# A float32 decoder on one Trainium2 core: half of retention's output product as block pairs, gates kept in HBM, head norms by quarters, and fourteen weight units with low parts from ScalarE and an accumulating transfer

## The chip, the cores and the metric

The kernel runs on one core of a Trainium2 chip. The metric is the device time of one execution in microseconds (us). TensorE is PE (its weight loads are PEld), VectorE is DVE, ScalarE is ACT, GpSimd is POOL, and SyncE, which issues most transfers, is SP.

## The reference

Two layers; 512 tokens; width 1024. The weights are float32. In each layer

```python
h = rmsnorm(x, g_mix)
aq, ak, av, rq, rk, rv, rg, ga, gb = split(h @ w_in)      # 5888 columns
A = sliding_window_attention(aq, ak, av, sinks)            # 8 heads, window 128
r = retention(rq, rk, rv)                                  # 4 heads of 256 columns
r = r * rsqrt(mean(r * r, per head) + EPS) * silu(rg)
mixed = sigmoid(ga) * (A @ w_a) + sigmoid(gb) * (r @ w_b)
x = x + mixed @ w_out
x = x + square(relu(rmsnorm(x, g_mlp) @ w_up)) @ w_down
```

and a last rmsnorm of x. The change touches r's norm, sigmoid(gb), r @ w_b, and how the weights of gb, w_b and w_out are prepared.

## The kernel before

**Layout and precision.** Activations stand transposed: a chunk is 128 features on partitions by 512 tokens. A matmul takes a 128x128 block of weights as its stationary side and 512 tokens as its moving side. Each float32 operand is split in two parts of a reduced format: `hi` is a rounded copy that ScalarE writes (L257), `lo` is the rest, raw minus hi, by VectorE (L258). A product then takes three matmuls, hi·hi, hi·lo and lo·hi (`products`, L303 to L305). PE pays three times for every product, and each weight costs one ACT and one DVE pass.

**Weight units.** All weights come in units of 128x1024 (512 KB), in the order that `unit_order` writes out. `load_until` issues the loads on SP three units ahead into `raw` tiles, `split_until` makes hi and lo, and `unit` hands a unit to the product that uses it and has the next ones split. The pool `wpool` holds three each of raw, hi and lo: a unit's hi and lo can be written only when the unit three before it has been read by its last matmul. PSUM has eight banks: five for `ps_mm` and three for `ps_aux`.

**Kinds of products.** `chunk` takes one unit and gives one output chunk: 8 blocks × 3 = 24 matmuls of 512 columns. `group` takes four units and gives four chunks together in four banks: 96 matmuls of 512. `two_chunks` takes two units for two chunks. `narrow_pair` (L563) gives two output chunks from two weight units by seven block products instead of eight: the units' halves and sums and differences of them (`load_part` and `add_part`, which make four parts, on DVE) meet halves of the input and sums and differences of those (`sum_input`, `form_of`: "forms"). Each of its seven products has 4 blocks × 3 matmuls over 256 tokens, 84 matmuls of 256 columns in all. Before the change, w_out's last six chunks and most of w_up's are made as pairs.

**Retention and gates.** `retention(pair)` is a generator that runs in the background of the projection chunks: `advance` lets it take a step at fixed points (twice a chunk, times a rate). Per head it makes scores, outputs, a norm (`inverse_rms`, L405: a matmul with ones sums the squares, ACT takes the root of 128x512, DVE the reciprocal of 128x512) and `finish` (L996), which multiplies by the norm and by silu(rg) and splits the result into the moving side of w_b. The queue's order after retention's second half is: rg chunks 4–7; gates 0–3 (`chunk` with `gate`, L835: DVE multiplies by rstd, ACT takes the sigmoid); the w_b `group` for chunks 0–3; gates 4–7; w_b chunks 4–7; w_out `two_chunks`; w_out's pairs; then w_up. `put_mixed` (L1088) multiplies w_b's output by the gate, adds the attention branch and splits the sum. `chunk` order within the gates is permuted by CROSSED, so that pairs of chunks lie beside each other.

**Order.** The program is written in this order, and a scheduler settles the order of instructions on each engine when the kernel is built. Each engine then runs its list in order and waits at an instruction whose operands aren't there, with all behind it.

Of the kernel before, what the change touches and what calls it, by code (L numbers as in the profile page):

```python
# [18 lines left out]
P = 128  # L19
# [33 lines left out]
BETWEEN = (0, 2, 4, 5)  # L53
H = T // 2
CROSSED = (0, 1, 4, 5, 2, 3, 6, 7)


def unit_order():

    def plain(name, *at):  # L60
        return [(name, i) for i in range(*at)]

    def pairs(src, *firsts):
        return [("pair", j, part, src) for j in firsts for part in range(4)]

    order = plain("w_in", 26) + plain("w_a", 4) + plain("w_in", 26, 42)
    order += plain("w_b", 4) + plain("w_in", 42, 46) + plain("w_b", 4, 8)
    order += plain("w_out", 2) + pairs("w_out", 2, 4, 6)
    for what, q, i in mlp_sequence():
        if what == "first":  # L70
            order += plain("w_up", 4)
        elif what == "pair":
            order += pairs("w_up", 8 * q + 2 * i)
        elif what == "down":
            order += plain("w_down", 8 * q + 2 * i, 8 * q + 2 * i + 2)
        else:
            order += plain("w_down", 8 * q, 8 * q + 8)
    return order
# [43 lines left out]
def view(slot):  # L122
    return slot[0][:, slot[1], :]
# [3 lines left out]
def decoder(ctx, tc, xT, x_first, w_in, w_a, w_b, w_out, w_up, w_down, tables, decay, band, triangles, g_last, out):  # L127
# [33 lines left out]
    xhl = const.tile([P, 2, KD, T], F32R, name="xhl")  # L161
    xh, xl = xhl[:, 0], xhl[:, 1]
    slots = Slots([const.tile([P, 4, T], F32R, name=f"r{i}") for i in range(10)])
    spill = dram.tile([P, KD, T], F32, name="spill")


    order = [(layer, *u) for layer in range(DEPTH) for u in unit_order()]
    raws, parts, homes = {}, {}, []
    state = {"next": 0, "loaded": 0, "split": 0}

    def halves(i):

        return (slice(0, UNIT // 2), slice(UNIT // 2, UNIT)) if i < 3 else (slice(0, UNIT),)
# [59 lines left out]
    def split_until(n):  # L233
        while state["split"] < min(n, len(order)):
            i = state["split"]
            load_until(i + 3)
            paired = order[i][1] == "pair"
            if paired:
                add_part(i)
            raw = raws[i]  # L240
            if homes and i >= len(order) - len(homes):
                home = homes[len(order) - 1 - i]
                hi, lo = (home[:, 2 * a : 2 * a + 2, :].rearrange("p a t -> p (a t)") for a in range(2))
            else:


                first = (ASIDE, ASIDE) if paired else (0, 0)
                if paired and order[i][4] == "w_up" and wide(order[i][2]):
                    first = (ASIDE, 0)
                hi, lo = (  # L250
                    wpool.tile([P, UNIT + P], F32R, tag=n, name=n)[:, a : a + UNIT] for n, a in zip(("hi", "lo"), first)
                )
            for at in (LEFT,) if paired and order[i][3] == 3 else halves(i):
                if i == 0 and at.start == 0:
                    nc.vector.tensor_copy(hi[:, at], raw[:, at])
                else:
                    nc.scalar.activation(hi[:, at], raw[:, at], AF.Copy)  # L257
                last_low[:] = [nc.vector.tensor_tensor(lo[:, at], raw[:, at], f32(hi[:, at]), ALU.subtract).ins]  # L258
# [57 lines left out]
    xs = [(xh[:, k, :], xl[:, k, :]) for k in range(KD)]  # L316

    background = []
    credit = [0.0]
# [70 lines left out]
    def sum_parts(acc, folded=True):  # L390
# [11 lines left out]
        split(sh, sl, acc)  # L402
        return [sh, sl]

    def inverse_rms(both, n, dest):  # L405

        ps = bank(ps_aux, "ssq")
        for i, part in enumerate(both):
            nc.tensor.matmul(ps, ones, part, start=i == 0, stop=i == len(both) - 1)
        nc.scalar.activation(dest, ps, AF.Sqrt, bias=eps, scale=1.0 / n)  # L410
        nc.vector.reciprocal(dest, dest)
# [2 lines left out]

    def scaled_input(k, which):

        split(xh[:, k, :], xl[:, k, :], x[:, k, :], gain[:, which * KD + k : which * KD + k + 1])

    def squared_input(k, which):
        if k == 0:  # L420
# [94 lines left out]
    def layer_body(layer):  # L515
# [40 lines left out]

        def block(half, tokens):
            at = slice(tokens * H, tokens * H + H)
            return [xhl[:, :, k, at] for k in range(4 * half, 4 * half + 4)]

        FIRST, SECOND = slice(0, H), slice(H, T)

# [310 lines left out]
        def values(pair):  # L873

            banks = [bank(ps_mm, "rv") for _ in range(NB)]
            for u in range(4):
                hi, lo = unit("w_in", layer)
                for j in range(2):
                    k = 2 * u + j
                    cols = slice(j * T, (j + 1) * T)  # L880
                    for b, ps in enumerate(banks):
                        at = slice(b * P, (b + 1) * P)
                        products(
                            ps, [((xh[:, k, at], xl[:, k, at]), (hi[:, cols], lo[:, cols]))], k == 0, k == KD - 1
                        )
# [6 lines left out]
        rg, rg_next = {}, {}  # L892

        def put_rg(i):
            def put(ps):
                if i % 2 == 0:
                    two = big("z")
# [22 lines left out]
        class Head:  # L920
# [85 lines left out]
        def retention(pair):  # L1006
# [23 lines left out]
            for head in two:  # L1030
                head.finish()
                yield

        qk(0, PACE)
        for i in range(4):
# [36 lines left out]
        gates, gate_tiles = [], []  # L1072

        def gate_tile(c):
            if c % 2 == 0:
                two = big("gb")
                gate_tiles.append(two)
                gates.extend(two[:, j, :] for j in range(2))
# [7 lines left out]
        ms = {}  # L1086

        def put_mixed(c):  # L1088
            def put(ps):
                m = gates[c]  # L1090
                nc.vector.tensor_tensor(m, ps, m, ALU.mult)
                nc.vector.tensor_tensor(m, m, mixed[CROSSED[c]], ALU.add)
                hi, lo = slots.one(), slots.one()
                split(view(hi), view(lo), m)
                ms[CROSSED[c]] = (hi, lo)
# [22 lines left out]
        source = xT if layer == 0 else spill  # L1118
        for c in range(KD):
            nc.sync.dma_start(x[:, c, :], source[:, c, :])  # L1120

        def next_input(c):
            scaled_input(c, g_mlp)
# [63 lines left out]
        def wide_pair(first, close, pool, step):  # L1187
# [30 lines left out]
            part = unit("pair", layer)  # L1218
            multiply(a, part, True, block(0, 0))
            if first:  # L1220
                nc.tensor.matmul(b, part[0][:, :P], xh[:, 0, :], start=True, stop=True)
# [69 lines left out]
        for what, q, i in mlp_sequence():  # L1291
            if what == "first":
                late = group("w_up", layer, xs, [put_up] * 4, first_hooks())
            elif what == "pair":
                pair(q, i, late)
                if (q, i) == (3, 3):
                    for t, _ in homes_x:
                        slots.give(*t[1])
            elif what == "down":
# [3 lines left out]
            elif layer == DEPTH - 1:  # L1303
                end(layer, up[q])
            else:
                all_of(group("w_down", layer, up[q], [put_down(c, True) for c in range(4)]))
                for c in range(4, KD):
                    chunk("w_down", layer, up[q], put_down(c, True))
                slots.give(*up_slots[q])

    scaled_input(0, 0)
    split_until(1)
    for u in (2, 3):
# [77 lines left out]
    return units + [_swapped(u) if i % 2 else u for i, u in enumerate(_units_chunks(w, 2 * P + r(D - 2 * P)))]  # L1391


def _up_units(w):

    units = _units_group(w, np.arange(T))
# [51 lines left out]
def _laid_out(x, g_mix, w_in, sinks, w_a, w_b, w_out, g_mlp, w_up, w_down, g_final):  # L1448
# [13 lines left out]
        "w_b": _stack(w_b, lambda w: _half_grouped(w[:, _crossed(r(D))])),  # L1462
# [27 lines left out]
```

## Time and profile before

| | us |
|---|---|
| median of 3 runs | 1479.55 |
| lowest and highest | 1479.36, 1480.13 |
| profiled execution | 1479.77 |
| its span | 1478.0 |
| PE busy in it | 1469.1 |
| ACT busy | 786.5 |

The profile is of one execution. A row of the windows view gives busy time of each engine in a stretch, with the number of instructions. A row of the timeline gives start, duration, engine, line, operation, out<-in and shapes; `[0.55 <-PE mm]` at its end is idle time before it and what ended it. Matmuls overlap one another, so their pace is read from start to start, not from the durations. In groups the figures behind the bar are total busy time, mean of one in ns, and the idle time before them with its releasers. In the transfers' rows the last figure is the median from issue to landing.

### The profile page before, as it was taken

To read this page: it belongs to the slowest core of one execution; us is meant where nothing else is said; L and a number is where in the kernel's file an instruction comes from. 1 tells how busy PE (TensorE), PEld (TensorE's weight loads), DVE (VectorE), ACT (ScalarE), POOL (GpSimd) and SP (SyncE) were. 2 spreads that over 40 slices of the span, in tenths; PEclk is the share of its full clock that TensorE was granted. 3 is DMA by queue.
4 is the path that set the end of the run, shared out by engine and by line. 5 is a ranking of instruction groups with operands and counts; after the bars stand their busy time and mean duration, and the time that the engine had idled before them with its cause. 6 is when DMAs were issued, how large, how long until landed. Compare 5 with 4: busy or idle time off the path is not lost.

```text
span 1478.0 us, 19499 instructions
## 1 busy us (share of the span) xinstructions
PE 1469.1 (99%) x7322; PEld 1245.8 (84%) x7322; DVE 1144.0 (77%) x1864; ACT 786.5 (53%) x1250; POOL 3.8 (0%) x14
## 2 busy tenths in 40 slices
PE   9999999999999999999999999999999999999998
PEld 7888888888988888888888888888889888888887
DVE  7998668776998787776678975786779977878763
ACT  7656355643674445444456743556347654444553
POOL 0000000000000000000000000000000000000000
PEclk9999999999999999999999999999999999999999
DMA  6422322244323332333543233232433333333341
GB/s 226 136 86 86 93 82 89 75 125 128 92 81 114 100 114 93 105 103 114 167 129 91 86 98 87 87 100 76 135 93 105 102 95 99 115 103 110 90 140 57
DMA packets 52845, 155.58 MB, mean 105 GB/s; under 512 B 6416, under 2 KB 6544, under 8 KB 52752
## 3 DMA queue, kind: packets, MB, share of 16 engines
q1 hardware_dynamic: 52464, 153.83, 33.8%
q8 instruction: 57, 0.93, 0.3%
q10 hardware_dynamic: 288, 0.52, 0.1%
q14 instruction: 36, 0.29, 0.1%
HBM read 147.51 MB, written 4.19 MB: 103 GB/s over the span
## 4 chain that ended last, share of the span: by engine, by line
PE 91%; issue 5%; DVE 3%; DMA 1%; ACT 0%; POOLq 0%; SPq 0%; DVEq 0%
PE mm L305 21%; PE mm L303 21%; PE mm L304 21%; PE mm L1196 10%; PE mm L1197 5%; PE rv L303 2%; PE rv L305 2%; PE rv L304 2%; DVE lo L258 1%; PE score L776 1%; PE r L303 1%; PE r L305 1%; PE r L304 1%; PE pT L731 0%; PE pv L758 0%
## 5 line engine op out<-in xcount | busy, mean ns | idle before, releaser
L257 ACT ACTIVATE hi<-raw 128x1024 fp32r<-128x1024 f32 (+1 forms) x326 | 327.8, 1006 | 410.3 <-PE mm L304 210.9
L258 DVE TENSOR_TENSOR lo<-raw,hi 128x1024 fp32r<-128x1024 f32 (+1 forms) x327 | 377.6, 1156 | 125.9 <-ACT hi L257 122.4
L304 PE MATMUL mm<-r,hi 128*128 128x512 f32 (+1 forms) x824 | 298.6, 363 | 0.0
L303 PE MATMUL mm<-r,hi 128*128 128x512 f32 (+1 forms) x824 | 295.2, 364 | 0.0
L305 PE MATMUL mm<-r,lo 128*128 128x512 f32 (+1 forms) x824 | 293.3, 363 | 1.3 <-DVE lo L258 1.2
L304 PE MATMUL mm<-xhl,hi 128*128 128x512 f32 (+1 forms) x696 | 268.4, 388 | 0.0
L303 PE MATMUL mm<-xhl,hi 128*128 128x512 f32 (+1 forms) x696 | 268.2, 387 | 0.0
L305 PE MATMUL mm<-xhl,lo 128*128 128x512 f32 (+1 forms) x696 | 265.2, 388 | 0.0
L305 PEld LDWEIGHTS mm<-r,lo 128*128 128x128 f32 x824 | 154.1, 188 | 27.3 <-DVE lo L258 2.5
L304 PEld LDWEIGHTS mm<-r,hi 128*128 128x128 f32 x824 | 154.6, 188 | 23.9
L303 PEld LDWEIGHTS mm<-r,hi 128*128 128x128 f32 x824 | 154.2, 188 | 24.3
L303 PEld LDWEIGHTS mm<-xhl,hi 128*128 128x128 f32 x696 | 130.7, 188 | 25.6 <-ACT xhl L313 0.5
L305 PEld LDWEIGHTS mm<-xhl,lo 128*128 128x128 f32 x696 | 130.7, 188 | 24.7
L304 PEld LDWEIGHTS mm<-xhl,hi 128*128 128x128 f32 x696 | 130.8, 188 | 24.5
L1196 PE MATMUL mm<-r,hi 128*128 128x512 f32 x416 | 146.4, 391 | 0.0
L1197 PE MATMUL mm<-r,lo 128*128 128x256 f32 x416 | 115.4, 277 | 0.3 <-DVE lo L258 0.2
L1196 PE MATMUL mm<-xhl,hi 128*128 128x512 f32 x312 | 110.1, 391 | 0.0
L1196 PEld LDWEIGHTS mm<-r,hi 128*128 128x128 f32 x416 | 78.1, 188 | 16.3
L1197 PE MATMUL mm<-xhl,lo 128*128 128x256 f32 x312 | 86.6, 278 | 0.9 <-DVE lo L258 0.9
L1197 PEld LDWEIGHTS mm<-r,lo 128*128 128x128 f32 x416 | 78.1, 188 | 2.4 <-DVE lo L258 1.2
L1196 PEld LDWEIGHTS mm<-xhl,hi 128*128 128x128 f32 x312 | 58.6, 188 | 12.0
L1197 PEld LDWEIGHTS mm<-xhl,lo 128*128 128x128 f32 x312 | 58.6, 188 | 2.8 <-DVE lo L258 1.6
(261 smaller groups left out, 2051.9 us busy)
## 6 DMA issues: line engine op xcount, KB each, us to landing
raw<-w_in_in SPq DMA_DIRECT2D x89, 512.0 KB, 3.6
raw<-w_down_in SPq DMA_DIRECT2D x64, 512.0 KB, 3.6
raw<-w_up_in SPq DMA_DIRECT2D x36, 512.0 KB, 3.6
raw<-w_up_in SPq DMA_DIRECT2D x56, 256.0 KB, 2.8
raw<-w_b_in SPq DMA_DIRECT2D x16, 512.0 KB, 3.6
raw<-w_out_in SPq DMA_DIRECT2D x10, 512.0 KB, 3.6
raw<-w_a_in SPq DMA_DIRECT2D x8, 512.0 KB, 3.5
x<-xT_in SPq DMA_DIRECT2D x15, 256.0 KB, 3.1
```

The lines of the kernel that those rows point to most:

```text
L257: nc.scalar.activation(hi[:, at], raw[:, at], AF.Copy)
L258: last_low[:] = [nc.vector.tensor_tensor(lo[:, at], raw[:, at], f32(hi[:, at]), ALU.subtract).ins]
L303: nc.tensor.matmul(ps, ah, bh, start=start and i == 0, stop=False, **more)
L304: nc.tensor.matmul(ps, ah, bl, start=False, stop=False, **more)
L305: nc.tensor.matmul(ps, al, bh, start=False, stop=stop and i == n - 1, **more)
L776: nc.tensor.matmul(ps[:, g * w : (g + 1) * w], q_s[g][:, c, at], part[:, keys], start=i == 0, stop=i == 1)
L1196: nc.tensor.matmul(both, hi[:, c], m, start=start and k == 0, stop=False, **more)
L1197: nc.tensor.matmul(ps[:, :H], lo[:, c], m[:, 0, :], start=False, stop=k == 3 and start, **more)
```

## The change

- **w_b chunks 0–3** are made as two block pairs with `narrow_pair` (`mixed_pair`) in place of the `group`. Their forms of r are summed when each half of retention is finished.
- **Gates**: all eight gate chunks come before w_b, at an advance rate of 1.25. Two at a time they are written to HBM (`aside`) and read back when w_b uses them.
- **The tile `xhl`**, constant before, becomes slots that are given back after the gates and taken again.
- **Head norms**: `inverse_rms_apart` takes a head's root as four pieces of 32x128 on ACT, the reciprocal of one 128x128, writes the row of 512 to HBM, and reads it back spread over 128 partitions.
- **ADDED units**: for the gates' eight units, w_b 4–7 and w_out 0–1, ACT writes hi, then lo = −hi; then a transfer that POOL issues adds the weight from HBM to lo. DVE's subtraction is dropped. These weights are read from HBM twice.

```diff
+ADDED = {"w_b": range(4, 8), "w_in": range(38, 46), "w_out": range(2)}
...
-    order = plain("w_in", 26) + plain("w_a", 4) + plain("w_in", 26, 42)
-    order += plain("w_b", 4) + plain("w_in", 42, 46) + plain("w_b", 4, 8)
+    order = plain("w_in", 26) + plain("w_a", 4) + plain("w_in", 26, 46)
+    order += pairs("w_b", 0, 2) + plain("w_b", 4, 8)
     order += plain("w_out", 2) + pairs("w_out", 2, 4, 6)
...
+            if adds(i):
+                nc.scalar.activation(hi, raw, AF.Copy)
+                last_low[:] = [nc.scalar.activation(lo, f32(hi), AF.Copy, scale=-1.0).ins]
+                nc.gpsimd.dma_start(lo, weights[order[i][1]][order[i][0], order[i][2]], accum_op=ALU.add)
+                raws.pop(i)
+                parts[i] = (hi, lo)
+                state["split"] += 1
+                continue
...
+    def inverse_rms_apart(both, n, dest):
+
+        ps = bank(ps_aux, "ssq")
+        for i, part in enumerate(both):
+            nc.tensor.matmul(ps, ones, part, start=i == 0, stop=i == len(both) - 1)
+        own = temp("own")[:, :P]
+        for b in range(NB):
+            rows, cols = slice(32 * b, 32 * b + 32), slice(b * P, (b + 1) * P)
+            nc.scalar.activation(own[rows, :], ps[rows, cols], AF.Sqrt, bias=eps[rows, :], scale=1.0 / n)
+        nc.vector.reciprocal(own, own)
+        row = dram.tile([NB, P], F32, tag="row", name="row", bufs=2)
+        nc.sync.dma_start(row, own[0 : P : P // NB, :])
+        nc.sync.dma_start(dest, row.rearrange("b t -> (b t)").unsqueeze(0).broadcast_to([P, T]))
...
-                inverse_rms(self.parts, RET_V, self.inv)
+                inverse_rms_apart(self.parts, RET_V, self.inv)
...
+            for i in (pair, pair + 2):
+                homes_r[i] = forms_home()
+                by_form_r[i] = homes_r[i][1]
+            sum_input(by_form_r, [rg_tiles[2 * pair], rg_tiles[2 * pair + 1]], 2 * pair)
...
         for i in range(4, 8):
-            chunk("w_in", layer, xs, put_rg(i))
...
-        for c in range(4):
-            gate_tile(c)
-            chunk("w_in", layer, xs, gate(gates[c]))
+            chunk("w_in", layer, xs, put_rg(i), 1.25)
+        gates, gate_tiles, fresh = [], [], []
+
+        def put_aside(c):
+            def put(ps):
+                if c % 2 == 0:
+                    fresh[:] = [big("gb")]
+                gate(fresh[0][:, c % 2, :])(ps)
+                if c % 2:
+                    nc.sync.dma_start(aside[:, c - 1 : c + 1, :], fresh[0])
+
+            return put
+
+        for c in range(KD):
+            chunk("w_in", layer, xs, put_aside(c), 1.25)
         drain()
+        old_input()
+
+        def gate_tile():
+            c = len(gates)
+            two = big("gate")
+            nc.sync.dma_start(two, aside[:, c : c + 2, :])
+            gate_tiles.append(two)
+            gates.extend(two[:, j, :] for j in range(2))
...
-        all_of(group("w_b", layer, rT, [put_mixed(c) for c in range(4)]))
+
+        def mixed_pair(c):
+
+            gate_tile()
+            two, own = gate_tiles[c // 2], CROSSED[c]
+
+            def put(i, at, src, z):
+                return nc.vector.tensor_tensor(two[:, i, at], two[:, i, at], src, ALU.mult)
+
+            narrow_pair(ps_aux if c == 0 else ps_mm, lambda ins: None, form_of(by_form_r), block_r, put)
+            nc.vector.tensor_tensor(two, two, x[:, own : own + 2, :], ALU.add)
+            for i in range(2):
+                split_mixed(c + i, gates[c + i])
...
+        for c in (0, 2):
+            mixed_pair(c)
+        for t, _ in homes_r:
+            slots.give(*t[1])
...
         for c in range(4, KD):
-            gate_tile(c)
-            chunk("w_in", layer, xs, gate(gates[c]))
-        for c in range(4, KD):
+            if c % 2 == 0:
+                gate_tile()
             chunk("w_b", layer, rT, put_mixed(c))
```

More of the change, by code (lines that the diff above doesn't have):

```diff
@@ L160, in decoder @@
     x = little_x[:, P:].rearrange("p (k t) -> p k t", t=T)
[L161 to L164, printed above, removed]
+    slots = Slots([const.tile([P, 4, T], F32R, name=f"r{i}") for i in range(14)])
+    spill, aside = (dram.tile([P, KD, T], F32, name=n) for n in ("spill", "aside"))
     order = [(layer, *u) for layer in range(DEPTH) for u in unit_order()]
@@ L169, in decoder, with adds @@
     state = {"next": 0, "loaded": 0, "split": 0}
+    def adds(i):
+        return order[i][1] in ADDED and order[i][2] in ADDED[order[i][1]]
     def halves(i):
@@ L314, in split, with new_input, old_input @@
             nc.vector.scalar_tensor_tensor(lo, src, scale, f32(hi), ALU.mult, ALU.subtract)
-    xs = [(xh[:, k, :], xl[:, k, :]) for k in range(KD)]
+    xs, x_homes = [], []
+    def new_input():
+        x_homes[:] = [slots.four() for _ in range(KD // 2)]
+        xs[:] = [(x_homes[k // 2][0][:, k % 2, :], x_homes[k // 2][0][:, 2 + k % 2, :]) for k in range(KD)]
+    def old_input():
+        for t in x_homes:
+            slots.give(*t[1])
     background = []
@@ L415, in scaled_input @@
     def scaled_input(k, which):
-        split(xh[:, k, :], xl[:, k, :], x[:, k, :], gain[:, which * KD + k : which * KD + k + 1])
+        split(*xs[k], x[:, k, :], gain[:, which * KD + k : which * KD + k + 1])
     def squared_input(k, which):
@@ L558, in block @@
             at = slice(tokens * H, tokens * H + H)
-            return [xhl[:, :, k, at] for k in range(4 * half, 4 * half + 4)]
+            return [x_homes[k // 2][0][:, k % 2 :: 2, at] for k in range(4 * half, 4 * half + 4)]
         FIRST, SECOND = slice(0, H), slice(H, T)
@@ L896, in put @@
                 if i % 2 == 0:
-                    two = big("z")
+                    two = rg_tiles[i // 2] = big("z")
                     rg[i], rg_next[i + 1] = two[:, 0, :], two[:, 1, :]
@@ L1070, in layer_body, with split_mixed @@
         for i in range(4, 8):
-            chunk("w_in", layer, xs, put_rg(i))
[L1072 to L1078, printed above, removed]
-        for c in range(4):
-            gate_tile(c)
-            chunk("w_in", layer, xs, gate(gates[c]))
-        drain()
+            chunk("w_in", layer, xs, put_rg(i), 1.25)
[10 more added lines that the diff above has]
+            chunk("w_in", layer, xs, put_aside(c), 1.25)
+        drain()
+        old_input()
[5 more added lines that the diff above has]
+            gates.extend(two[:, j, :] for j in range(2))
         ms = {}
+        def split_mixed(c, m):
+            hi, lo = slots.one(), slots.one()
+            split(view(hi), view(lo), m)
+            ms[CROSSED[c]] = (hi, lo)
         def put_mixed(c):
@@ L1092, in put, with block_r @@
                 nc.vector.tensor_tensor(m, m, mixed[CROSSED[c]], ALU.add)
-                hi, lo = slots.one(), slots.one()
-                split(view(hi), view(lo), m)
-                ms[CROSSED[c]] = (hi, lo)
+                split_mixed(c, m)
             return put
         rT = [tuple(view(s) for s in ret[k]) for k in range(KD)]
-        all_of(group("w_b", layer, rT, [put_mixed(c) for c in range(4)]))
+        def mixed_pair(c):
[7 more added lines that the diff above has]
+                split_mixed(c + i, gates[c + i])
+        def block_r(half, tokens):
+            at = slice(tokens * H, tokens * H + H)
+            return [tuple(m[:, at] for m in rT[CROSSED[k]]) for k in range(4 * half, 4 * half + 4)]
+        for c in (0, 2):
+            mixed_pair(c)
+        for t, _ in homes_r:
+            slots.give(*t[1])
         homes_m = [forms_home(), None, forms_home(), None]
@@ L1220, in wide_pair @@
             if first:
-                nc.tensor.matmul(b, part[0][:, :P], xh[:, 0, :], start=True, stop=True)
+                nc.tensor.matmul(b, part[0][:, :P], xs[0][0], start=True, stop=True)
             ins = nc.vector.tensor_copy(b, a).ins if close else nc.scalar.activation(b, a, AF.Copy).ins
@@ L1461, in _laid_out @@
         "w_a": _stack(w_a, lambda w: _units_chunks(w[wa_rows], r(D))),
-        "w_b": _stack(w_b, lambda w: _half_grouped(w[:, _crossed(r(D))])),
+        "w_b": _stack(w_b, _ret_units),
         "w_out": _stack(w_out, _out_units),
```

13 lines of the change are left out of this document (11 added, 2 removed).

## The prediction

> **What bounds the kernel now.** First the page: busy times and the summary of the chain that ended last.
>
> ```profile
> span 1478.0 us, 19499 instructions
> PE 1469.1 (99%) x7322; PEld 1245.8 (84%) x7322; DVE 1144.0 (77%) x1864; ACT 786.5 (53%) x1250; POOL 3.8 (0%) x14
> PE 91%; issue 5%; DVE 3%; DMA 1%; ACT 0%; POOLq 0%; SPq 0%; DVEq 0%
> ```
>
> TensorE works 99% of the span, so time goes down by fewer PE microseconds and up by every new PE wait. POOL does nothing. Then PE's waits, and the busy times by stage in layer 0: the matmuls of w_b's group (296.5 to 318), gates 4–7 (to 340), w_b 4–7 (to 362), w_out.
>
> ```profile
> PE mm L305 <- DVE lo L258: 1.2, 2, 0.6
> PE mm L1197 <- DVE lo L258: 1.1, 3, 0.5
> ```
> ```profile
> 296.50:318.00 21.50, 21.50 (x96) 17.83 (x95) 12.31 (x12) 7.75 (x9) 0.00 (x0) 1.00 0.32 97
> 318.00:340.00 22.00, 22.00 (x98) 18.21 (x97) 18.58 (x25) 11.40 (x14) 0.00 (x0) 1.00 0.53 158
> 340.00:362.00 22.00, 22.00 (x98) 18.20 (x97) 13.09 (x17) 6.67 (x8) 0.00 (x0) 1.00 0.34 103
> 382.00:392.00 10.00, 9.69 (x83) 9.48 (x81) 10.00 (x16) 6.94 (x12) 0.00 (x0) 1.00 0.26 60
> 392.00:402.00 10.00, 9.72 (x81) 9.61 (x82) 9.96 (x17) 6.18 (x11) 0.00 (x0) 1.00 0.44 146
> ```
>
> PE waits only 2.3 us, always for a low part (`lo`) of a weight from VectorE. The columns are PE, PEld, DVE, ACT, POOL busy, clock (1.00, undisturbed), DMA share and GB/s. Where w_b and the gates run, PE is full and DVE has room; only in w_out's block pairs is DVE full. The changed stage is bounded by PE, with some 9 us of DVE slack in 21.5.
>
> **The matmuls (a gain).** The rates come from PE's timeline at the end of w_out's pairs and in w_up:
>
> ```profile
> 399.74 0.28 PE L303 MATMUL mm<-r,hi 128*128 128x256 f32 x1
> ...
> 402.21 0.40 PE L303 MATMUL mm<-xhl,hi 128*128 128x512 f32 x1
> ...
> 405.21 0.39 PE L304 MATMUL mm<-xhl,hi 128*128 128x512 f32 x1
> ...
> 407.02 0.39 PE L303 MATMUL mm<-xhl,hi 128*128 128x512 f32 x1
> ```
>
> From 399.74 to 402.21 lie 21 matmuls of 256 columns: 0.1176 us each, start to start. From 405.21 to 407.02 lie 8 of 512: 0.2263. Per layer the change removes the group's 4 units × 2 × 4 × 3 = 96 of 512 (21.7 us) and adds 2 pairs × 7 products × 4 blocks × 3 = 168 of 256 (19.8 us). Gain 1.95 a layer, **−3.9** in all. The number of gate matmuls doesn't change.
>
> **Work that moves off or onto idle time.** The groups by form:
>
> ```profile
> L258 DVE TENSOR_TENSOR lo<-raw,hi 128x1024 fp32r<-128x1024 f32 x287 | 350.5, 1221 | 122.3 <-ACT hi L257 118.8 <-PE ret L305 2.4
> L311 DVE TENSOR_TENSOR r<-z,r 128x512 fp32r<-128x512 f32 x64 | 42.9, 686 | 2.8 <-ACT r L310 2.6
> L411 DVE RECIPROCAL inv<-inv 128x512 f32<-128x512 f32 x8 | 26.8, 3353 | 10.4 <-ACT inv L410 10.4
> L257 ACT ACTIVATE hi<-raw 128x1024 fp32r<-128x1024 f32 x287 | 303.7, 1058 | 398.0 <-PE mm L304 208.9 <-PE mm L1196 101.2 <-issue 50.6
> ```
>
> - Fourteen units a layer lose DVE's subtraction (14 × 1.22 = 17 us off DVE) and gain a second ScalarE copy (14 × 1.06 = 15 us on ACT). Eight gates and six others take 76 us of PE; ACT worked about half of that stage (11.40 of 22.00), so per unit of 24 × 0.2263 = 5.4 us it carries two copies and a sigmoid, under 3 us. Nothing by itself; its cover is ACT's idle half.
> - The pairs add DVE sums (four 128x512 of weights and some of `r` per pair, under 0.7 each). They fit into the slack above, except at one place (below).
> - Gates to HBM and back: four writes and four reads of 512 KB a layer on SP. In the new order the first read stands behind the write of gates 4–5 and is wanted after the first pair's fourth product, by my count 4 us after it has landed at 3.6 us a piece. Nothing; if that cover went, DVE's gate product would come late and the PSUM bank after it.
>
> **Norms by a quarter and through HBM (a small loss).** The rows beside it: the old chain of a head, and the transfers.
>
> ```profile
> 301.45 0.69 ACT L410 ACTIVATE inv<-ssq,x 128x512 f32<-128x512 f32 x1 [2.10 <-PE ssq L409]
> 302.18 3.35 DVE L411 RECIPROCAL inv<-inv 128x512 f32<-128x512 f32 x1 [3.39 <-ACT inv L410]
> ...
> 306.52 1.28 DVE L1000 TENSOR_TENSOR z<-z,inv 128x512 f32<-128x512 f32 x2
> 307.72 1.29 DVE L1001 TENSOR_TENSOR z<-rr,z 128x512 f32<-128x512 f32 x2
> 308.93 1.22 DVE L258 TENSOR_TENSOR lo<-raw,hi 128x1024 fp32r<-128x1024 f32 x1
> 310.06 1.28 DVE L311 TENSOR_TENSOR r<-z,r 128x512 fp32r<-128x512 f32 x2
> ```
> ```profile
> raw<-w_up_in SPq DMA_DIRECT2D x56, 256.0 KB, 2.8
> raw<-w_b_in SPq DMA_DIRECT2D x16, 512.0 KB, 3.6
> spill<-x SPq DMA_DIRECT2D x8, 256.0 KB, 2.3
> x<-spill SPq DMA_DIRECT2D x8, 256.0 KB, 3.0
> r<-r SPq DMA_DIRECT2D x8, 64.0 KB, 3.6
> ```
>
> Start to start, DVE steps cost 0.60 (306.52 to 307.72 holds two of 512) and 1.13 (308.93 to 310.06; I count 1.15) for 1024. Old: 0.7 + 3.4 = 4 us. New, estimated: four roots (1.9), a quarter of the reciprocal (3.35/4 = 0.84) with a weight sum ahead of it, done 3.5 us after the square sum; the row to HBM like `spill<-x`, 2.3; back like `x<-spill`, 3.0: landed at 9. DVE stands in its order at the multiplication by it, and behind that wait the last head's seven steps, four gates' evacuations (the last gate's PSUM bank waits for the first of these) and the low parts of the first pair. In layer 0's new order the last square sum stands 64 matmuls ahead of gate 7 and 87 (19.7 us) ahead of the first pair's first low part. From 9 on, in DVE's new order: the head's seven steps and gate 2's evacuation, 8 × 0.60, so its bank is free at 13.8 (wanted at 14.3); five more of 0.60 and 1.15 give the first `lo` at 17.95 (wanted 19.7); two of each kind the second at 21.5 (22.5); the third, behind a form's low part, two sums and ScalarE's copy of them, at 26.2 (25.3: 0.9 late); the second pair's first, behind three of 0.60 and two of 256 columns at 0.33 (446.18 to 446.51, below), at 29.8 (28.2 + 0.9: another 0.75). So 1.7 in layer 0. In layer 1 the square sum stands 13 matmuls, 3 us, earlier: nothing. **+1.7**, between 0 (a trip shorter by 1 us does it) and 4.2 (both ways like `r<-r`, 7.2 in place of 5.3: +1.9 in layer 0, +0.6 in layer 1). I take the rows of 256 KB to and from HBM: the same two directions; a row of 2 KB that is spread over 128 partitions is nearest to them in what lands.
>
> **Low parts by an accumulating transfer (the disputed term).** Nothing in this trace runs such a transfer. Its nearest scene is where pairs of w_up give way to a plain unit:
>
> ```profile
> 442.89 1.05 ACT L257 ACTIVATE hi<-raw 128x1024 fp32r<-128x1024 f32 x1
> ...
> 445.04 1.22 DVE L258 TENSOR_TENSOR lo<-raw,hi 128x1024 fp32r<-128x1024 f32 x1
> ...
> 445.08 0.28 PE L1197 MATMUL mm<-xhl,lo 128*128 128x256 f32 x1
> ...
> 445.19 0.40 PE L303 MATMUL mm<-r,hi 128*128 128x512 f32 x1
> ...
> 445.28 1.06 ACT L257 ACTIVATE hi<-raw 128x1024 fp32r<-128x1024 f32 x1 [0.55 <-PE mm L1196]
> ...
> 445.89 0.40 PE L304 MATMUL mm<-r,hi 128*128 128x512 f32 x1
> 446.18 0.42 DVE L1208 TENSOR_TENSOR eu<-eu,mm 128x256 f32<-128x256 f32 x1
> ...
> 446.32 0.73 PE L305 MATMUL mm<-r,lo 128*128 128x512 f32 x2
> 446.51 0.42 DVE L1203 TENSOR_TENSOR z<-mm,side 128x256 f32<-128x256 f32 x1
> ```
>
> Here a low part took 3.4 us from the start of its high part (442.89) to its first use (446.32), and PE still waited 0.2 (445.89 + 0.23 to 446.32). The change makes such a scene behind the second pair of w_b: unit w_b 4 takes the buffers of that pair's second weight part. In the new order PE then has 36 matmuls of 256 and four of 512 ahead of w_b 4's first low part: 36 × 0.1176 + 4 × 0.2263 = 5.1 us. Off go 0.2 to start (445.28 above followed a matmul begun at 445.08), two copies of 1.06: 2.8 us are left for a transfer of 512 KB from issue to landing, X. The PE stall is X − 2.8, once a layer, in both.
>
> X from below: a plain 512 KB load, 3.6, stall 0.8. A second stream through the engines (the target is read too) costs what 256 KB more cost, twice: 2 × (3.6 − 2.8) = 1.6, so 5.2. In the order the raw load of the next unit is issued about 1 us earlier, another 512 KB: partly shared, +0.8. I take **X = 6.0**, stall 3.2, **+6.4** in all. From above: two plain loads end to end and the shared one, 2 × 3.6 + 1.6 = 8.8: 6.0 a layer, 12.0.
>
> The Trainium skill ("DMA: Bandwidth & Descriptors", the section "Anatomy of one DMA — SWDGE (gpsimd) path") gives transfers issued from GpSimd 2.0 us and bytes at 436 GB/s, an estimate of 3.2 us for 512 KB, below every plain row here; by it the sum would be 1478.4 in place of 1484.0.
>
> The other thirteen units have slack: three `lo` buffers turn over in 3 × 5.4 = 16.3 us, of which one unit's reading (5.4) and ACT (2.4) take 7.8, so X up to 8.5 costs nothing.
>
> **Sum.** Against the profiled execution's own 1479.8 (span 1478.0 and 1.8 around it, 0.2 above the median): 1479.8 − 3.9 + 1.7 + 6.4 = 1484.0; against the median 1483.8.
>
> **Rivals.**
> 1. *The transfer lands as fast as a plain load* (X under 4.5). For it: POOL and its queue are idle and the stage's DMA share is 0.34. Against it: each word is read twice. At X = 3.6: 1479.8 − 3.9 + 1.7 + 1.6 = 1479.2, not slower; without the norm's stall 1477.5. If DVE, freed of six subtractions just before w_out, also loses the pairs' wait there (0.6 a time by the waits, two times), 1476.3. It decides below X = 2.8 + 1.95 = 4.75, where a layer's stall eats its gain. Chance 0.30, of which 0.12 ends faster.
> 2. *The transfer is slow and all fourteen units starve* (X of 9 and more), because descriptors or the add run late. At X = 10: 7.2 behind the pairs, and (7.8 + 10 − 16.3)/3 = 0.5 for each of 8 gates, 11.2 a layer: 1479.8 − 3.9 + 1.7 + 22.4 = 1500. For it: nothing here shows a POOL transfer, and DVE is 84% busy in the gates' stage (18.58 of 22). Against it: a plain load is far below. Chance 0.10. The Trainium skill ("SBUF — State Buffer", the trap "DVE blocks DMA") has VectorE's two-port operations hold up the writing of such descriptors; no run shows it yet.
> 3. *The norm's trip is long, and DVE becomes the bound in front of the pairs*: both ways like `r<-r` (4.2), and the second pair's weights, whose buffer DVE frees late, land 1.6 later a layer (3.2): 1479.8 − 3.9 + 7.4 + 6.4 = 1489.7. For it: VectorE waits in order. Against it: the margins above are near 0.5 to 2 us only in layer 0. Chance 0.08.
> 4. *The change doesn't do what it says*: the pairs' PE gain is lost because PEld (9.5 of 10 in pairs) paces them. Against it: 0.1176 was measured there. With it 1487.9; chance 0.04.
>
> **How the numbers follow.** The forecast (X from 4.5 to 7.5) has 0.48 and its own range is 1481 to 1487. About 0.2%, 3 us, is what a measurement here can tell: faster means below 1476.6, slower above 1482.5. Faster: 0.12 of rival 1 and 0.03 of the forecast's with DVE's relief and no norm stall, 0.15. Same: the rest of rival 1 (0.18) and the forecast where X is below 5.2 (0.10), 0.28. Slower: 0.57. The range takes in rival 1's lower end and X = 8.8 (1479.8 − 3.9 + 1.7 + 12.0 = 1489.6): 1476.0 to 1490.0, leaving out rival 2 and slivers of the others.
>
> **What would show it.** Right: a PE wait of 2 to 5 us once a layer at w_b 4's first low matmul, released by a POOL transfer; 256-wide steps of 0.118 in the new pairs; PE's waits on `lo` elsewhere under 2 us a layer; 28 POOL transfers landing 5 to 7 us after issue. Wrong: no PE wait there (rival 1), waits at each gate unit (rival 2), or long PE waits for DVE's `lo` in the first pair (rival 3).

## The result, and the profile after

The changed kernel takes 1500.3 us (median of 4 runs, 1498.0 to 1504.4) against 1479.6 (4 runs, 1479.4 to 1480.1): ratio 1.0141, interval 1.0128 to 1.0154. It is 20.7 us slower. The forecast, 1483.8, had the sign right and a fifth of the size. The new kernel's runs also spread over 6 us, the old one's over less than 1.

The page of the changed kernel, its busy times, the summary of the chain that ended last and two rows of the transfer queues (packets, MB, share of the sixteen engines' span):

```profile
span 1500.4 us, 20088 instructions
PE 1474.7 (98%) x7466; PEld 1253.5 (84%) x7466; DVE 1132.8 (76%) x1892; ACT 837.9 (56%) x1330; POOL 28.1 (2%) x42
PE 84%; issue 7%; DVE 5%; DMA 3%; ACT 1%; POOLq 0%; SPq 0%; DVEq 0%; ACTq 0%
q1 hardware_dynamic: 56560, 164.33, 34.1%
q0 software_dynamic: 4032, 14.68, 5.8%
```

Transfers now hold 3% of the chain. The software queue is the 28 adding transfers: 14.68 MB, 5.8% of 1500.4 us of all sixteen engines, 3.1 us for each 512 KB. The hardware queue moved 164.33 MB in 34.1%, 1.6 us for each 512 KB. A transfer that adds took about twice the engines' time of a plain one.

What PE waited for (total us, times, longest):

```profile
PE mm L316 <- DMA lo<-w_b_in: 9.6, 2, 5.4
PE mm L314 <- DVE gb L871: 3.3, 2, 2.3
PE mm L316 <- DVE lo L269: 1.7, 4, 0.6
PE mm L314 <- ACT hi L268: 1.6, 1, 1.6
...
PE mm L316 <- DMA lo<-w_in_in: 0.2, 1, 0.2
```

Two long waits for w_b 4's low part, one a layer, as forecast; two for gates' evacuations by DVE and one for a first-pair weight, all where the last head's norm makes its trip; almost none at the gate units.

The transfers, median from issue to landing:

```profile
lo<-w_in_in POOLq DMA_DIRECT2D x16, 512.0 KB, 6.6
...
gate<-aside SPq DMA_DIRECT2D x8, 512.0 KB, 8.8
lo<-w_b_in POOLq DMA_DIRECT2D x8, 512.0 KB, 9.0
...
raw<-w_out_in SPq DMA_DIRECT2D x12, 256.0 KB, 12.8
...
inv<-row SPq DMA_DIRECT2D x8, 256.0 KB, 4.0
```

The trace has the landing of every POOL transfer, but of few that SP issued, so three of these rows rest on little: `gate<-aside` on two reads (4.8 us for a first pair's, 12.8 beside the adding transfers), `raw<-w_out_in` on three loads (12.8 and 13.2 behind the pairs, 3.2 later), `inv<-row` on one. Even so the loads of w_out's pairs, which nobody changed and whose median was 3.1 us before, took four times as long behind w_b's pairs. Not all of that comes from the adding transfers: with none of them (the first experiment below) two such loads took 6.8 and 7.8 us. Now the place behind the second pair in layer 0, from POOL's and PE's timelines:

```profile
341.95 0.86 POOL L259 DMA_DIRECT2D lo<-w_b_in  x1 [35.85 <-ACT lo L258]
344.62 0.86 POOL L259 DMA_DIRECT2D lo<-w_b_in  x1 [1.81 <-ACT lo L258]
346.97 0.86 POOL L259 DMA_DIRECT2D lo<-w_b_in  x1 [1.48 <-ACT lo L258]
```
```profile
344.53 0.40 PE L315 MATMUL mm<-r,hi 128*128 128x512 f32 x1
350.33 0.80 PE L316 MATMUL mm<-r,lo 128*128 128x512 f32 x1 [5.41 <-DMA lo<-w_b_in]
350.92 0.63 PE L314 MATMUL mm<-r,hi 128*128 128x512 f32 x1
351.35 0.63 PE L315 MATMUL mm<-r,hi 128*128 128x512 f32 x1
351.78 0.63 PE L316 MATMUL mm<-r,lo 128*128 128x512 f32 x1
```

Issued at 341.95, used at 350.33: X was 8.4 us. PE stood from 344.53 + 0.23 for 5.6 us. In layer 1 X was 8.4 us as well; there PE stood 0.9 us for a high part by ScalarE and then 4.4 for the low part. Then something new: from 350.92 the matmuls start 0.43 us apart in place of 0.23. The windows of the same stretch show it in the last column but two, the granted clock (with DMA share and GB/s behind it):

```profile
340.00:344.00 4.00, 3.95 (x32) 3.51 (x32) 2.82 (x6) 3.42 (x4) 0.86 (x1) 1.00 0.89 267
344.00:348.00 4.00, 0.93 (x6) 0.48 (x5) 3.44 (x5) 3.77 (x6) 1.73 (x2) 0.94 0.97 237
348.00:352.00 4.00, 1.67 (x4) 1.39 (x5) 3.58 (x5) 1.61 (x2) 0.00 (x0) 0.50 1.05 270
352.00:356.00 4.00, 4.00 (x14) 3.12 (x14) 0.00 (x0) 0.00 (x0) 0.00 (x0) 0.71 1.05 273
```

The clock falls to 0.50 after the wait, and the sixteen DMA engines are all busy (0.89 to 1.05, where the stage was at 0.34 before).

**Where 22.4 us of span went.** Over all matmuls behind the start, counted at the two paces of the prediction: the new shapes are 3.9 us less; starts that came late add 29.7 us where they added 9.4 before; 31 matmuls at 0.43 add 0.2 each, 6.2. Sum −3.9 + 20.3 + 6.2 = 22.6.

The second place, the norm's trip of the last head in layer 0, as PE, DVE and SP saw it:

```profile
299.19 0.39 PE L429 MATMUL ssq<-sh,ones 128*128 128x512 f32 x1
```
```profile
303.15 0.69 DVE L226 TENSOR_TENSOR raw<-raw 128x512 f32<-128x512 f32 x1 [5.38 <-DMA raw<-w_b_in]
303.76 0.95 DVE L434 RECIPROCAL own<-own 128x128 f32<-128x128 f32 x1
311.48 1.29 DVE L1034 TENSOR_TENSOR z<-z,inv 128x512 f32<-128x512 f32 x2 [6.78 <-DMA inv<-row]
```
```profile
304.73 0.50 SPq L436 DMA_DIRECT2D row<-own  x1
306.46 0.32 SPq L437 DMA_DIRECT2D inv<-row  x1
```

12.3 us from square sum to use, not 9.0: the sum of the first pair's weights, ahead of the reciprocal on DVE, waited for its load (about 2 us), and the way back took 5.0, not 3.0. In layer 1 it was 15.1 us. The DMA engines were 0.83 and 0.84 busy during the two trips. PE then stood 1.8 and 1.2 us in layer 0, and 2.5 in layer 1, for banks and weights that DVE gave late.

### The profile page after: what moved, and what is told of

Its sections match the earlier page's. It is cut to its first block, busy times and chain, and to the rows that moved or that the text cites. A ratio compares the mean times of both kernels' runs of the same rounds, so it can differ in the third digit from the quotient of the medians.

```text
span 1500.4 us, 20088 instructions
## 1 busy us (share of the span) xinstructions
PE 1474.7 (98%) x7466; PEld 1253.5 (84%) x7466; DVE 1132.8 (76%) x1892; ACT 837.9 (56%) x1330; POOL 28.1 (2%) x42
## 3 DMA queue, kind: packets, MB, share of 16 engines
q1 hardware_dynamic: 56560, 164.33, 34.1%
q0 software_dynamic: 4032, 14.68, 5.8%
## 4 chain that ended last, share of the span: by engine, by line
PE 84%; issue 7%; DVE 5%; DMA 3%; ACT 1%; POOLq 0%; SPq 0%; DVEq 0%; ACTq 0%
PE mm L316 19%; PE mm L314 19%; PE mm L315 19%; PE mm L1272 10%; PE mm L1273 5%; PE rv L314 2%; PE rv L316 2%; PE rv L315 2%; DVE lo L269 1%; DMA lo<-w_b_in 1%; DMA inv<-row 1%; PE score L810 1%; DVE r L322 1%; DMA raw<-w_b_in 1%; PE r L314 1%
## 5 line engine op out<-in xcount | busy, mean ns | idle before, releaser
L314 PE MATMUL mm<-r,hi 128*128 128x512 f32 (+1 forms) x1568 | 573.8, 369 | 6.3 <-DVE gb L871 3.3
L316 PE MATMUL mm<-r,lo 128*128 128x512 f32 (+1 forms) x1568 | 565.8, 369 | 11.6 <-DMA lo<-w_b_in 9.6
L315 PE MATMUL mm<-r,hi 128*128 128x512 f32 (+1 forms) x1568 | 575.1, 368 | 0.0
L316 PEld LDWEIGHTS mm<-r,lo 128*128 128x128 f32 x1568 | 295.3, 189 | 62.5 <-DMA lo<-w_b_in 10.5
L314 PEld LDWEIGHTS mm<-r,hi 128*128 128x128 f32 x1568 | 295.8, 189 | 56.2 <-ACT r L321 2.7
L315 PEld LDWEIGHTS mm<-r,hi 128*128 128x128 f32 x1568 | 295.8, 189 | 46.2
L1272 PE MATMUL mm<-r,hi 128*128 128x512 f32 x728 | 251.9, 391 | 0.0
L1273 PE MATMUL mm<-r,lo 128*128 128x256 f32 x728 | 200.3, 277 | 1.2 <-DVE lo L269 1.1
L1272 PEld LDWEIGHTS mm<-r,hi 128*128 128x128 f32 x728 | 136.5, 188 | 28.3
L1273 PEld LDWEIGHTS mm<-r,lo 128*128 128x128 f32 x728 | 136.7, 188 | 5.2 <-DVE lo L269 2.8
L321 ACT ACTIVATE r<-z 128x512 fp32r<-128x512 f32 x64 | 38.6, 621 | 24.5 <-DVE z L1035 24.5
L315 PE MATMUL rv<-lo,r 128*128 128x512 f32 x128 | 49.8, 389 | 0.0
L316 PE MATMUL rv<-hi,r 128*128 128x512 f32 x128 | 49.5, 389 | 0.0
L314 PE MATMUL rv<-hi,r 128*128 128x512 f32 x128 | 49.4, 390 | 0.0
L322 DVE TENSOR_TENSOR r<-z,r 128x512 fp32r<-128x512 f32 x64 | 43.0, 686 | 2.8 <-ACT r L321 2.6
L226 DVE TENSOR_TENSOR raw<-raw 128x512 f32<-128x512 f32 x38 | 26.1, 688 | 20.3 <-DMA raw<-w_b_in 9.0
```

Of the source, the lines that this page charges most:

```text
L314: nc.tensor.matmul(ps, ah, bh, start=start and i == 0, stop=False, **more)
L315: nc.tensor.matmul(ps, ah, bl, start=False, stop=False, **more)
L316: nc.tensor.matmul(ps, al, bh, start=False, stop=stop and i == n - 1, **more)
L321: nc.scalar.activation(hi, src, AF.Copy)
L322: nc.vector.tensor_tensor(lo, src, f32(hi), ALU.subtract)
L1272: nc.tensor.matmul(both, hi[:, c], m, start=start and k == 0, stop=False, **more)
```

## The experiments

All times beside runs of the kernel before on the same chip, 1479.6 to 1480.0 us.

**No added units.**

```diff
-ADDED = {"w_b": range(4, 8), "w_in": range(38, 46), "w_out": range(2)}
+ADDED = {}
```

> The changed kernel with no unit on the accumulating transfer: all fourteen units a layer take their low parts from VectorE again; pairs, gates in HBM and quartered norms stay. Theory (transfers that add are the root: each takes twice the DMA engines' time, so w_b 4 is late by 5.6 us and the norm's trip by 2 to 3 us): the wait at w_b 4 goes altogether, the norm's trip is 9 to 10 us, PE waits for it at most 1 us a layer; time 1476 to 1480 us. Rival (the norm's trip is long by itself and VectorE, with 17 us more a layer, is the bound in front of the pairs): PE waits 3 us and more a layer there, 1484 to 1490 us.

1480.2 us (1479.6 to 1483.1), ratio 1.0003 (0.9994 to 1.0013). The waits at w_b 4 and for gates' banks are gone. The trip:

```profile
300.32 0.39 PE L429 MATMUL ssq<-sh,ones 128*128 128x512 f32 x1
```
```profile
302.26 0.95 DVE L434 RECIPROCAL own<-own 128x128 f32<-128x128 f32 x1 [3.05 <-ACT own L433]
...
308.52 1.29 DVE L1034 TENSOR_TENSOR z<-z,inv 128x512 f32<-128x512 f32 x2 [3.59 <-DMA inv<-row]
```

8.2 us here and 9.1 in layer 1, with the DMA engines 0.34 and 0.29 busy. The time lies 0.2 us above the theory's range: waits that PE had not before, of 0.2 to 0.5 us each at the new pairs and at w_out's first (14.1 us of late starts in all, 4.7 more than before), take back what the matmuls gain.

**The old norm, added units kept.**

```diff
-                inverse_rms_apart(self.parts, RET_V, self.inv)
+                inverse_rms(self.parts, RET_V, self.inv)
```

> The changed kernel with the four head norms a layer as before (128x512 root and reciprocal, nothing through HBM); the fourteen added units stay. Theory (norm trip costs about 4 us a layer by the waits in the trace, w_b 4's transfer about 8): 1490 to 1494 us, the wait of about 5.5 us at w_b 4's first low part unchanged, no wait for gates' banks ahead of the pairs. Rival (the two share one cause, the transfers, and the old reciprocal of 3.35 us stops VectorE as long): 1498 to 1502 us.

1494.3 us, ratio 1.0096 (1.0081 to 1.0111): the theory, 0.3 us above its range. PE's two waits for w_b 4's low part stay (9.5 us of idle in all, 9.6 in the changed kernel), those for gates' banks are gone. **Neither** (both edits):

> No added units and the old norms: block pairs and gates in HBM alone. Theory: PE keeps most of the 3.9 us of fewer matmul time: 1475.5 to 1479 us. Rival (VectorE is the bound without the two reliefs; that is what they are needed for): waits for VectorE's low parts in the first pair of 3 us and more a layer, 1482 us and more.

1488.0 us, ratio 1.0053 (1.0036 to 1.0070): the rival's time. Its PE waits:

```profile
PE mm L316 <- DVE lo L269: 3.0, 5, 0.8
PE mm L314 <- ACT r L321: 3.0, 2, 1.8
```

With the old reciprocals on DVE the first pair's operands are late, more by the last head's forms of r (the second row) than by low parts: two of the first row's five waits are at w_out's pairs and are in all these kernels. The four corners, in us:

| | norm on DVE | norm by HBM |
|---|---|---|
| no added units | 1488.0 | 1480.2 |
| fourteen added units a layer | 1494.3 | 1500.3 |

The trip through HBM gains 7.8 us with quiet transfers and loses 6.0 with the adding ones. It isn't good or bad by itself.

**Which gates.** Only the eight gate units added:

> Only the eight gate units a layer take the transfer; w_b 4 to 7 and w_out 0 to 1 get their low parts from VectorE. Theory: the wait behind the second pair goes (16 us with the slow matmuls that follow it, both layers), the norm's stays: 1482 to 1486 us. Rival (VectorE, busy with the pairs, is late for w_b 4 as well): a wait of 2 us and more on VectorE's low part there, 1488 us and more.

1489.1 us, ratio 1.0060 (1.0045 to 1.0075): more than the theory's 1482 to 1486, since the trip's waits came with smaller ones at w_out's pairs (1.3 and 1.2 us in layer 0). The rival's wait on DVE for w_b 4 didn't appear. Then four of the eight each:

```diff
+ADDED = {"w_in": range(38, 42)}     # x4_early_gates
+ADDED = {"w_in": range(42, 46)}     # x6_late_gates
```

> Only the first four gate units a layer (the ones before the last head's norm makes its trip) take the transfer. Theory (the trip is late because such transfers are in flight with it): the last trip of a layer takes 8 to 10 us from square sum to use, as without added units, and the time is within 2 us of that kernel, 1479 to 1482 us. Rival (the eight gate units cost what they cost by ScalarE's second copy or by the loads' order, whichever four they are): half of the 8.8 us that all eight cost, 1484 to 1486 us.

> Only the last four gate units a layer take the transfer; they are in flight with the last head's trip. Theory: the trip takes 11 to 15 us, PE waits 2 us and more a layer for a gate's bank ahead of the pairs, 1486 to 1490 us. Rival: half of what all eight cost, 1484 to 1486 us, and not more than the first four.

1478.5 us (ratio 0.9994, 0.9984 to 1.0003) and 1487.7 us (1.0055, 1.0040 to 1.0070). The last head's trip took 8.7 and 9.0 us with the early four, 12.1 and 13.1 with the late four. The DMA engines were 0.40 busy during these trips with the early four, and 0.89 and 0.97 with the late four. One adding transfer in flight did little (7.8 and 9.4 us for the third head's trips with the early four); with the late four it was three. The rival, that each half costs the same, is out. PE's longest wait ahead of the pairs with the late four was, though, for a first-pair weight (1.7 us in layer 0), not for a gate's bank (0.6).

**What w_b 4's transfer costs.** Alone of its kind:

```diff
+ADDED = {"w_b": range(4, 5)}
```

> Only w_b 4, the first plain unit behind the pairs, takes the transfer, so that no other such transfer is in flight. Theory A (a transfer that adds takes 8.4 us because two more of its kind, weight loads and the gates' reads share the engines): it lands in 5 to 6 us, the PE wait there is 2.2 to 3.2 us, time 1484 to 1489 us with the slow matmuls behind it. Theory B (8.4 us is its own length): the wait is 5 to 5.6 us, 1491 to 1494 us.

1485.7 us (1483.5 to 1490.5), ratio 1.0044 (1.0030 to 1.0058), but by another way than expected. The two transfers landed in 8.2 and 7.1 us, between the theories; PE waited only 0.35 us there, because the scheduler put other matmuls ahead. The time in the trace went at w_out's first pair (3.6 and 2.3 us, for a copy on ScalarE). That execution took 1490.5 us, 4.8 above the median, so these waits are not the median's. As a test of the wait it is inconclusive; as a length it isn't: no other adding transfer was in flight, and it still took 7.1 and 8.2 us beside that place's plain loads. The shortest in any run, with one load beside it, took 5.1 to 5.5 us.

> Only w_b 4 to 7 take the transfer. Theory (of the 11.2 us that the six units behind the gates cost, w_out's two cost nothing and w_b's all; three units behind a pair start together): waits of 4 to 5.6 us a layer at w_b's low parts with slow matmuls behind them, 1488 to 1493 us. Rival (they cost that only together with the gates' late reads and w_out's transfers): under 1485 us.

With all of w_b 4 to 7 and no others: 1496.9 us, ratio 1.0118 (1.0104 to 1.0132), 16.6 above no added units and more than I expected. PE's waits:

```profile
PE mm L316 <- DMA lo<-w_b_in: 7.8, 2, 4.5
PE mm L314 <- ACT hi L257: 4.7, 2, 3.0
```

The second row is a new wait. In this kernel's order two matmuls on w_b 6's high part stand ahead of w_b 4's first low part; ScalarE made that high part late, because its load was:

```profile
342.25 1.06 ACT L257 ACTIVATE hi<-raw 128x1024 fp32r<-128x1024 f32 x1 [2.38 <-DMA raw<-w_b_in]
```

The plain loads suffer in the burst as well. So w_b's four units alone are enough for more than the 11.2 us between 1500.3 and 1489.1.

> Only w_out 0 and 1 take the transfer. Theory: away from the norm's trip and from w_b 4 each lands in 6 to 9 us, inside the two units of lead; nothing is lost, and VectorE is a little earlier at w_out's pairs: 1478.5 to 1481 us. Rival (it shares the burst of loads for x and w_out's pairs there, which is what hurt with w_b 6 and 7): 1484 us and more.

w_out 0 and 1 alone: 1479.7 us, ratio 1.0000 (0.9991 to 1.0009). Free, as the theory had it.

> w_b 6 and 7 and w_out 0 and 1 take the transfer, ten units a layer are VectorE's again. Theory (a transfer of 6 to 9 us hides where two units of PE work lie ahead of it, and VectorE is then free for w_out's pairs): no wait at w_b's low parts, the waits at the first w_out pair (0.5 and 0.2 us a layer without added units) go, 1478.0 to 1480 us. Rival (the transfers slow the loads of w_out's pairs): waits there grow, 1481 us and more.

w_b 6 and 7 with w_out 0 and 1: 1495.3 us, ratio 1.0107 (1.0092 to 1.0122): my theory failed. Two units of lead weren't enough: in each layer the first three transfers, issued within 6 us, took 10.5 to 12.0 us. And they were not all that PE waited for:

```profile
353.61 0.69 DVE L1147 TENSOR_TENSOR gate<-mm,gate 128x512 f32<-128x512 f32 x1 [5.01 <-DMA gate<-aside]
```
```profile
354.36 0.79 PE L314 MATMUL mm<-r,hi 128*128 128x512 f32 x1 [2.12 <-DVE gate L1147]
```

DVE stood 5.0 us for a gate's read from HBM that was issued beside these transfers, and PE 2.3 us for the bank behind DVE's product (2.2 in layer 1). That is as much a layer as the wait for w_b 6's low part (2.5 and 2.4 us).

**PE's order and PE's clock.** Low products last in w_b 4:

> The changed kernel with w_b 4's matmuls in another order: the sixteen on its high part first, the eight on its low part last. PE has 12 x 0.2263 = 2.7 us more ahead of the first low part. Theory (the wait there is the landing time less PE's lead): it shrinks from 5.6 to about 2.9 us, w_b 5's low part, which lands about 4 us behind w_b 4's, is then waited for by about 1.2 us, and the time falls by 3 to 8 us (with the clock staying up), 1492 to 1497 us. Rival (the transfers finish together at the end of a burst whatever PE does): the waits only move, 1498 to 1503 us.

1499.3 us (1496.4 to 1502.4), ratio 1.0129 (1.0110 to 1.0148). The wait at w_b 4 shrank to 0.35 and 3.2 us, and new ones came at later transfers (1.9 us at w_b 5 in layer 0, 3.7 at w_out 0): the rival.

```diff
+        if fill:
+            spare = bank(ps_aux, "spare")
+            for _ in range(fill):
+                nc.tensor.matmul(spare, hi[:, :P], moving[0][0], start=True, stop=True)
         products(ps, pairs[: n // 2], True, False)
...
+            chunk("w_b", layer, rT, put_mixed(c), fill=22 if c == 4 else 0)
```

> The changed kernel with 22 matmuls of 512 columns more a layer into a spare PSUM bank, on w_b 4's high part, ahead of its first low part: 22 x 0.2263 = 5.0 us of PE work, the size of the wait there (5.6 us). The results of these matmuls are not used. Theory (the nine to fifteen matmuls at 0.43 us behind that wait are PE's clock, taken down by the wait itself): the wait shrinks to about 0.6 us, the slow matmuls behind it vanish, and the kernel is 4 to 5 us faster than the changed one, 1494 to 1497 us. Rival (the matmuls are slow because transfers fill the memory at that time): they stay at 0.43 us and the time stays 1498 to 1502 us.

1503.4 us (1499.9 to 1504.2), ratio 1.0154 (1.0139 to 1.0169). The clock part of the theory held, in the windows of the same place:

```profile
344.00:348.00 4.00, 4.00 (x23) 3.45 (x22) 0.00 (x0) 0.29 (x1) 0.86 (x1) 1.00 0.99 233
348.00:352.00 4.00, 4.00 (x22) 3.40 (x21) 3.23 (x5) 3.38 (x5) 0.86 (x1) 1.00 1.00 229
```

PE works through, the DMA engines are as busy as in the changed kernel, the clock stays 1.00, and no matmul behind it is slow (8 in all, at the norm's place, where there were 31). So the slow matmuls come from PE's idling, not from the busy DMA engines. The gain I had expected did not come: PE waited 2.0 us at a later unit (w_b 6) in layer 0 and still 1.8 at w_b 4 in layer 1, the 5.0 us of filling are work, and the time lies inside the spread of the changed kernel.

**The transfers in the kernel before.** The same fourteen units, no pairs, old norms and gates:

> The kernel before with the same fourteen units a layer on the accumulating transfer and nothing else: no pairs in w_b, norms and gates as before. Theory (the transfer costs only behind a pair or beside another trip through memory): plain units have two units of lead, no PE wait of a microsecond, 1478 to 1481 us. Rival (the transfers' load alone makes other transfers late): waits at gate units and at w_out's pairs, 1484 us and more.

1480.5 us, ratio 1.0005 (0.9995 to 1.0014), no wait for any of them:

```profile
lo<-w_in_in POOLq DMA_DIRECT2D x16, 512.0 KB, 6.3
...
lo<-w_b_in POOLq DMA_DIRECT2D x8, 512.0 KB, 7.1
...
lo<-w_out_in POOLq DMA_DIRECT2D x4, 512.0 KB, 7.4
```

Twenty-eight such transfers are free in that kernel, where each follows plain units and no two start less than 4.6 us apart. Full DMA engines alone cost nothing there: from 322 to 334 us they were 1.01 busy and PE worked through. Whether the lead, the spacing or the other loads make w_b 6's transfer harmless here and late in the run of w_b 6 and 7 was not tested one by one.

**The two harmless sets together.**

```diff
+ADDED = {"w_in": range(38, 42), "w_out": range(2)}
```

> The first four gate units and w_out 0 and 1 take the transfer, the other eight of the fourteen are VectorE's: the two sets that cost nothing alone. Theory (a transfer that adds is harmless where neither the norm's trip nor a unit behind a pair is near): no wait over 1 us anywhere, the small ones in the first pair and at w_out's first pair go, 1476.5 to 1478.5 us, faster than the kernel before. Rival (their gains overlap or the run-to-run spread eats them): 1479 to 1481 us.

1477.8 us (1476.9 to 1480.4), ratio 0.9989 (0.9980 to 0.9998): in the theory's range and 1.8 us under the kernel before, less than the 3 us that the prediction says a measurement here can tell. From the early four alone (0.9984 to 1.0003) it can't be told apart. The theory missed one thing: waits of 1.3 and 1.1 us at w_out's first pair are left (a copy on ScalarE).

## Why the prediction went wrong, by its own steps

- **The matmuls, −3.9**: right. 192 matmuls of 512 fewer and 336 of 256 more, at paces that held; rival 4 is out.
- **X − 2.8 behind the second pair**: the formula was right, the term mis-sized. X measured 8.4 in both layers where I took 6.0. The wait was 5.6 us in layer 0 (8.4 − 2.8 = 5.6); in layer 1 it was 5.3, of which 0.9 was for ScalarE's high part. My bound from above, 8.8, held. The step that failed is "another 512 KB: partly shared, +0.8". The 5.2 before it fits transfers with little beside them (5.1 to 5.5), but the sharing cost 3.2 us, not 0.8, and 1.9 to 3.0 of it are there when no other adding transfer is in flight (7.1 and 8.2). Three units behind a pair start their transfers within 5 us (341.95, 344.62, 346.97), and the gates' reads and w_out's loads start there as well; I had counted one load.
- **The norm's trip, +1.7**: the step that failed is the choice of `spill<-x` and `x<-spill` as prices, rows from stages with the DMA engines 0.47 and 0.43 busy. They hold when the adding transfers are elsewhere (8.2 to 9.1 against my 9.0); with three and four of them in flight and the engines 0.83 and 0.84 busy it was 12.3 and 15.1 us, and layer 1, where I took nothing, was the longer. I priced the two terms one by one, and the table of four corners shows that they aren't separate.
- **A PE wait costs its length**: a term put at nothing without a reason. It was never written down, but every price rested on it. 31 matmuls at half clock added 6.2 us, a third on top of the waits.
- **Thirteen units with slack to X = 8.5**: right for the gates and w_out (0.2 us of waits at gate units), though w_b 5 and 6 took up to 10.6.
- **Gates in HBM at nothing**: right for the read that I counted, a first pair's (4.8 us). I left out the third and fourth, which are issued beside w_b 4's adding transfers: one took 12.8 us and DVE waited 7.5 us at most. In the changed kernel PE's waits don't name them; in w_b 6 and 7's run they do, by 2.3 and 2.2 us, in the way that I had written (DVE's gate product late, the bank after it).
- **PE's waits before**: "only 2.3 us, always for a low part" leaves out 1.0 us at the program's start; no term uses it.
- **DVE's relief at w_out's pairs** (0.6 us a time in rival 1): did not happen; the wait of 0.76 us there is in both kernels and in the one before with added units.

Rival 2 had the right time, 1500, by the wrong way: the gates didn't starve, and X was under 9 at the unit that mattered. Rival 3 had a right mechanism, but I gave it 0.08 and left its cause, the transfers, in another rival. "Slower" came true through w_b 4, as forecast.

What stays open: why w_b's four units cost 16.6 us alone and all fourteen only 20.1. The order that the scheduler settles differs from kernel to kernel (w_b 6's place is one case), and I didn't hold it fixed.

## What to carry to other kernels

Price a transfer at the load of the place where it will run, not at its median elsewhere: add up what is issued within the same few microseconds, with an adding transfer counted twice. A trip through memory on a critical chain and a burst of extra transfers must be costed together; moving the extra transfers by four units was worth 9 us here. On an engine that is 99% busy, a wait of some microseconds can cost its length and then the slower clock behind it (6.2 us behind 20.3 here).

## What the runs showed of the hardware

- An accumulating transfer of 512 KB from HBM took 3.1 us of all sixteen engines, a plain one 1.6; it landed in 5.1 to 5.5 us with one load beside it, in 5.5 to 8.2 among the weight loads of the kernel before, and in up to 12.0 in a burst. POOL itself was busy 0.86 us for each.
- PE's clock was granted at 0.50 after a wait of 5.6 us, and at 0.60 after waits of 1.8 and 1.2 us with two matmuls between them; the slow starts went on for 3.4 to 6 us. One wait of 2.45 us in layer 1 had no slow matmul behind it. The Trainium skill ("TensorE: Matmul & The Clock Gate", Part 1 on the clock gate) has free-running windows of 3.4 us: one idle takes the clock to half, one busy brings it back. The slow starts' 3.4 to 6 us lie between one such window and two, which agrees. That 1.8 and 1.2 us of idling with two matmuls between them were enough, with no 3.4 us idle throughout, does not follow from it; here the measurement decides, and how much idling in a window is enough stays open.
